# Delta-net mixer: keys squared first, the pair scales on VectorE, half of the block copies on GpSimd, and the diagonal copies placed behind the E blocks

## The chip, the cores and the metric

The program runs on one core of one Trainium2 chip. The metric is the device time of one launch in microseconds (us), from arrays in HBM to the output in HBM. The engines named below are TensorE (PE; PEld is its weight load), VectorE (DVE), ScalarE (ACT), GpSimd (POOL) and SyncE (SP), which issues the transfers of the weights.

## The reference, cut to what matters

Two layers are computed, each a feed-forward block, a mixer and another feed-forward block, with an RMS norm before and behind each. D is 1024, there are 256 tokens in float32. The mixer of layer 1, a gated delta-net with 8 key heads and 16 value heads of width 128 and chunks of 64, is where the change lies:

```
q, k, v = silu(causal_conv4(x @ w_in))           # per channel, width 4
q, k    = l2norm(q), l2norm(k)                   # x * rsqrt(sum(x*x) + 1e-6), each repeated for 2 value heads
q       = q * 128 ** -0.5
decay   = exp(g[:, None] - g[None, :]) below and on the diagonal, 0 above    (g = cumulative log decay)
a       = strict lower part of (beta * k @ k.T) * decay
t_inv   = inverse of (eye + a)                   # one 64 x 64 triangular inverse per chunk and head
u, w    = t_inv @ (v * beta), t_inv @ (k * beta * exp(g))
then chunk by chunk: v_new = u - w @ state; o = q_g @ state + qk @ v_new; state = decayed state + k_tail.T @ v_new
out     = (rms_norm(o) * silu(z)) @ w_out
```

The kernel squares and sums q and k per head for the l2 norms, forms k @ k.T and k @ q.T for all heads, scales them by beta over the key's squared norm and by the decay, works with chunks of 128 tokens (one token tile), and inverts the strict triangles of all 32 pairs of value head and token tile together. The 1e-6 under the norm of q is carried into the output's RMS norm (the tile eq).

## The kernel before, in words

Every weight arrives in units of 512 KB (128 x 1024 float32) through SP's queue into one of 3 raw buffers. Each unit is split: ACT copies it to a rounded high part (whi, L119) and DVE subtracts that from the raw data for the low part (wlo, L121), into one of 8 buffer pairs. A product in float32 is three matmuls: high by high, low by high, high by low. They run nearly back to back on PE from the first microsecond to the last, and the delta-net's side work runs beside and between them.

What stands where is set twice. While the program is written, Python generators ("chains": the heads' chain kq_chain, invert, scan, v_pair, z_chain) are advanced by a ticker that is called every few projection matmuls, with written-out delays (KQ_WAIT 3, INV_WAIT 37, V_WAIT 4 ticks). Then a scheduler in the framework fixes one queue for each engine, by its own estimate of costs and priorities; issue_after(x) asks it to place an instruction behind x. On the chip each queue runs strictly in that order, and instructions wait on semaphores for data and for free buffers. So an edit on one line can move rows of other lines.

The part that the change touches, in the order of time (span of the delta-net mixer some 660 to 900 us of the profile):

- Convolutions and SiLU of the 16 q and k channels blocks: L584 (ACT) and three L586 (DVE) each, then SiLU L573 (ACT) for a head's k and q together. Their tiles are called kq.
- kq_chain, for each of 4 groups of 2 key heads. For each head PE transposes q and k into one PSUM bank (L618) and multiplies k by k and q into another (L621); both banks come from a pool of 4, called acc, so each bank is reused two heads later. ACT reads the first bank with the copies ktok (L624) and k1 (L625, from kq) and four squares with a running sum (L630, output "junk", sums in kss). Then the pair scales: POOL adds EPS to the sums (L634), DVE takes the reciprocal (L636, rk), POOL multiplies it with beta for the two token tiles (L639, dsc). POOL also makes the square root nk (L654), eq (L656) and wt (L658).
- For each token tile DVE writes four scaled products (L645, tile KQ, which frees the product banks), 8 for a group. For each tile four block copies on ACT (L652) pick the 32 x 32 diagonal blocks of KQ into one big tile blk for the inversion; 32 copies in all, 8 for a group.
- invert, once all four groups are through: DVE transposes blk (L669), then 31 steps of two DVE operations (L677, L679) invert all 32 x 32 blocks together, and two DVE transposes (L681, L683) bring the results back. POOL then copies the inverted blocks into E (L699, with a memset L700) for half 0 and half 1, and 32 diagonal blocks into KQ (L689). PE, ACT assemble the larger inverses from them (L707, L711, L718, L719, L732, L739).
- Meanwhile the projection goes on with z and then v. The v pairs pass through convolution (L584, L586), SiLU and transposes on PE (L757), and scan uses the inverses.

Of the kernel before, what the change touches and what calls it, by code (L numbers as in the profile page):

```python
# [7 lines left out]
F32 = mybir.dt.float32  # L8
F32R = mybir.dt.float32r
AF = mybir.ActivationFunctionType  # L10
ALU = mybir.AluOpType
PSUM = bass.MemoryType.PSUM

P = 128
# [35 lines left out]
def trunk_kernel(ctx: ExitStack, tc: tile.TileContext, x, norm_g, w_gu, w_dn, sc_in, sc_cw, sc_out,  # L50
# [425 lines left out]
    def gdn_proj(xh, xl, mid):  # L476
# [128 lines left out]
        def kq_chain():  # L605

            for gi in range(NG):
                ss = sp.tile([P, NT, 2, 2], F32, name="kss", bufs=2)
                k1 = slab([P, 2, 2, P], F32, "kq1")
                pkq = []  # L610
                for i in range(2):
# [11 lines left out]
                    pkq.append(pk)  # L623
                    S.activation(ktok[:, kh, :], tp[:, 0, 0, :], AF.Copy)  # L624
                    S.activation(k1[:, i, :, :], kq[kh][:, :, P:], AF.Copy)  # L625
                    kq1[kh] = k1[:, i, :, :]
                    for t in range(NT):
                        for c in range(2):
                            junk = sp.tile([P, 512], mybir.dt.bfloat16, name="junk", bufs=1)
                            S.activation(junk[:, 0:P], tp[:, t, c, :], AF.Square, accum_out=ss[:, t, c, i:i + 1])  # L630
# [3 lines left out]
                G.tensor_scalar(ss, ss, EPS, None, ALU.add)  # L634
                rk = sp.tile([P, NT, 2], F32, name="rk", bufs=2)
                V.reciprocal(rk, ss[:, :, 0, :])  # L636
                dd = small(f"dsc{gi}", 8).rearrange("p (t n) -> p t n", t=NT)
                for t in range(NT):
                    G.tensor_tensor(dd[:, t, :].rearrange("p (k v) -> p k v", k=2),  # L639
                                    beta[:, t, 4 * gi:4 * gi + 4].rearrange("p (k v) -> p k v", k=2),  # L640
                                    rk[:, t, :].unsqueeze(2).broadcast_to([P, 2, 2]), ALU.mult)
                for t in range(NT):
# [5 lines left out]
                    for b in range(4):  # L648
                        r = slice(b * B32, (b + 1) * B32)
                        o = Ld[r, :, 8 * gi + t:8 * gi + t + 7:2].rearrange("p i v -> p v i")  # L650
                        i_ = m[r, :, 0, b * B32:(b + 1) * B32]
                        S.activation(o, i_, AF.Copy)  # L652
                n = small(f"nk{gi}", 4).rearrange("p (t n) -> p t n", t=NT)
                G.tensor_tensor(n, ss[:, :, 0, :], phalf.rearrange("p (t n) -> p t n", t=NT), ALU.pow)  # L654
                q = small(f"eq{gi}", 4).rearrange("p (t n) -> p t n", t=NT)
                G.tensor_scalar(q, ss[:, :, 1, :], 128.0 * EPS, None, ALU.mult)  # L656
# [10 lines left out]
        def invert():  # L667
# [17 lines left out]
            for gi in range(NG):  # L685
                for t in range(NT):
                    for b in range(4):
                        r = slice(b * B32, (b + 1) * B32)
                        G.tensor_copy(KQ[gi][t][r, :, 0, r], Yd[r, 8 * gi + t:8 * gi + t + 7:2, :])  # L689
            yield INV_WAIT  # L690
            for half in range(2):
# [3 lines left out]
                for gi in gis:  # L695
# [4 lines left out]
                    G.memset(E[gi][0:B32, :, B32:], 0.0)  # L700
# [355 lines left out]
```

## Time and profile before

| | us |
|---|---|
| three timed runs | 1131.48, 1131.45, 1130.69 |
| median | 1131.45 |
| profiled execution | 1128.42 |
| its span, first to last instruction | 1126.5 |
| PE busy in the span | 1100.2 |
| DVE, ACT, POOL busy | 749.9, 651.8, 88.8 |

The profiled execution lies 3.03 us below the median of the timed runs, and 1.92 us of it are outside the span. The mean granted PE clock is 0.995 of full speed. PE is busy 98% of the span, so time can only go where PE idles, or where it runs at a lower clock; a matmul's busy time overlaps the next one's, so rows of matmuls are read by their starts. In a timeline row the first number is the start, the second the length of the piece, "xN" the instructions in it, and the bracket is the idle time of the engine before it and what ended that.

### The profile page before, as it was taken

How to read it: one execution, taken by the hardware profiler on the slowest of the kernel's cores; microseconds unless marked ns; L12 is line 12 of the kernel's file. 1: busy time of each engine (PE TensorE's matmuls, PEld its weight loads, DVE VectorE, ACT ScalarE, POOL GpSimd, SP SyncE). 2: the span in 40 equal slices, each digit the busy share in tenths (PEclk: the TensorE clock that was granted, in tenths of full speed). 3: DMA queues.
4: the chain of work that ended last, by engine and by line, in shares of the span. 5: the costliest groups of instructions: out<-in, count | busy, mean ns of one | idle time of the engine just before them, and what ended most of it. 6: DMA issues, size and time to landing. Idle time of an engine off the chain costs nothing.

```text
span 1126.5 us, 16842 instructions
## 1 busy us (share of the span) xinstructions
PE 1100.2 (98%) x6284; PEld 942.4 (84%) x6284; DVE 749.9 (67%) x1140; ACT 651.8 (58%) x1201; POOL 88.8 (8%) x167
## 2 busy tenths in 40 slices
PE   9999999999999999999999999889899999999997
PEld 6888887888788888788888877778899887888886
DVE  7776735687777663577765468768946557767543
ACT  6666535545556653556664358784587645666432
POOL 0100000000200000010000012110141212000000
PEclk9999999999999999999999999999999999999999
DMA  8755555656566565576555653327332355655552
GB/s 271 244 185 190 191 166 167 225 180 198 182 223 204 171 206 165 163 229 209 189 185 169 193 185 113 94 94 227 114 129 76 131 168 168 213 199 190 185 168 75
DMA packets 55955, 198.12 MB, mean 176 GB/s; under 512 B 6721, under 2 KB 7233, under 8 KB 55874
## 3 DMA queue, kind: packets, MB, share of 16 engines
q1 hardware_dynamic: 55728, 196.99, 54.2%
q8 instruction: 49, 0.80, 0.3%
q14 instruction: 32, 0.26, 0.1%
q10 hardware_dynamic: 146, 0.07, 0.0%
HBM read 195.99 MB, written 1.05 MB: 175 GB/s over the span
## 4 chain that ended last, share of the span: by engine, by line
PE 81%; DVE 7%; ACT 5%; DMA 3%; issue 2%; POOL 2%; SPq 0%; DVEq 0%; POOLq 0%; ACTq 0%
PE mm L298 27%; PE mm L301 14%; PE acc L324 7%; PE acc L325 7%; PE acc L323 7%; PE mm L221 3%; PE mm L222 3%; PE mm L225 3%; DVE wlo L121 2%; ACT whi L119 1%; ACT blk L652 1%; DVE kq L586 1%; PE mm L176 1%; ACT junk L147 1%; DMA raw<-in_w_gu 1%
## 5 line engine op out<-in xcount | busy, mean ns | idle before, releaser
L121 DVE TENSOR_TENSOR wlo<-raw,whi 128x1024 fp32r<-128x1024 f32 (+2 forms) x362 | 437.5, 1220 | 240.2 <-ACT whi L119 201.5
L119 ACT ACTIVATE whi<-raw 128x1024 fp32r<-128x1024 f32 (+2 forms) x362 | 376.1, 1051 | 224.3 <-PE acc L325 104.6
L298 PE MATMUL mm<-x,whi 128*128 128x512 f32 x1312 | 329.4, 393 | 0.0
L298 PEld LDWEIGHTS mm<-x,whi 128*128 128x128 f32 x1312 | 235.9, 189 | 42.4
L301 PEld LDWEIGHTS mm<-x,wlo 128*128 128x128 f32 x1312 | 179.0, 190 | 12.8
L301 PE MATMUL mm<-x,wlo 128*128 128x256 f32 x1312 | 182.9, 282 | 0.0
L323 PE MATMUL acc<-whi,hb 128*128 128x512 f32 x352 | 136.5, 388 | 0.0
L324 PE MATMUL acc<-wlo,hb 128*128 128x512 f32 x352 | 135.6, 385 | 0.3 <-DVE wlo L121 0.3
L325 PE MATMUL acc<-whi,hb 128*128 128x512 f32 x352 | 135.3, 385 | 0.0
L308 ACT ACTIVATE corr<-mm 128x256 f32<-128x256 f32 x164 | 61.2, 376 | 67.4 <-PE mm L301 65.6
L221 PE MATMUL mm<-whi,x 128*128 128x512 f32 (+1 forms) x240 | 94.4, 394 | 0.9 <-ACT x L178 0.7
L222 PE MATMUL mm<-wlo,x 128*128 128x512 f32 (+1 forms) x240 | 94.2, 393 | 0.7 <-DVE wlo L121 0.7
L225 PE MATMUL mm<-whi,x 128*128 128x512 f32 (+1 forms) x240 | 87.8, 389 | 0.2 <-DVE x L179 0.2
L324 PEld LDWEIGHTS acc<-wlo,hb 128*128 128x128 f32 x352 | 66.2, 188 | 13.8 <-DVE wlo L121 0.8
L323 PEld LDWEIGHTS acc<-whi,hb 128*128 128x128 f32 x352 | 66.2, 188 | 13.1
L325 PEld LDWEIGHTS acc<-whi,hb 128*128 128x128 f32 x352 | 66.1, 188 | 13.2
L154 POOL TENSOR_SCALAR rstd<-ss 128x1 f32<-128x1 f32 x24 | 12.3, 513 | 786.1 <-ACT junk L147 786.1
L278 PE MATMUL mm<-x,whi 128*128 128x256 f32 x200 | 59.7, 299 | 2.0 <-DVE kq L586 2.0
L279 PE MATMUL mm<-x,whi 128*128 128x256 f32 x200 | 58.4, 292 | 0.0
L280 PE MATMUL mm<-x,wlo 128*128 128x256 f32 x200 | 57.9, 289 | 0.0
L222 PEld LDWEIGHTS mm<-wlo,x 128*128 128x128 f32 x240 | 45.2, 188 | 11.2 <-DVE wlo L121 2.9
L221 PEld LDWEIGHTS mm<-whi,x 128*128 128x128 f32 x240 | 45.2, 188 | 11.1 <-ACT x L178 2.7
(216 smaller groups left out, 1238.3 us busy)
## 6 DMA issues: line engine op xcount, KB each, us to landing
raw<-in_w_gu SPq DMA_DIRECT2D x176, 512.0 KB, 4.2
raw<-in_w_dn SPq DMA_DIRECT2D x88, 512.0 KB, 3.6
raw<-in_sc_in SPq DMA_DIRECT2D x24, 512.0 KB, 4.1
raw<-in_gdn_z SPq DMA_DIRECT2D x16, 512.0 KB, 3.9
raw<-in_gdn_v SPq DMA_DIRECT2D x16, 512.0 KB, 4.2
raw<-in_gdn_out SPq DMA_DIRECT2D x16, 512.0 KB, 3.7
gamma<-in_norm_g SPq DMA_DIRECT2D x11, 512.0 KB, 5.4
raw<-in_gdn_a SPq DMA_DIRECT2D x9, 512.0 KB, 4.4
```

The lines of the kernel that those rows point to most:

```text
L119: S.activation(hi[:, r], raw[:, r], AF.Copy)
L121: newest[0] = V.tensor_tensor(lo[:, r], raw[:, r], hi[:, r], ALU.subtract).ins
L221: PE.matmul(pt, lhsT=xh[:, t, k, :], rhs=hi, start=(k == 0), stop=False)
L222: PE.matmul(pt, lhsT=xh[:, t, k, :], rhs=lo, start=False, stop=False)
L225: PE.matmul(pt, lhsT=xl[:, t, j, :], rhs=part(j)[0], start=False, stop=(j == KD - 1))
L278: PE.matmul(ptile, lhsT=hi, rhs=h2, start=(k == 0), stop=False)
L298: PE.matmul(flat, lhsT=part(k, 0), rhs=xx[:, k].rearrange("p h t q -> p (h t q)"), start=(k == 0), stop=False)
L301: PE.matmul(flat[:, T:], lhsT=part(k, 1), rhs=xx[:, k, 0].rearrange("p t q -> p (t q)"), start=False, stop=(k == KD - 1))
L308: S.activation(c, pt[:, 1, :], AF.Copy)
L323: PE.matmul(o, lhsT=yh(c, t), rhs=hi[:, r], start=(c == 0), stop=False)
L324: PE.matmul(o, lhsT=yh(c, t), rhs=lo[:, r], start=False, stop=False)
L325: i = PE.matmul(o, lhsT=yl(c, t), rhs=hi[:, r], start=False, stop=(c == n - 1)).ins
```

## The change

Four edits, all in the delta-net mixer:

1. The four squares of a head stand ahead of the copies ktok and k1, and the two of the keys ahead of the two of the queries. The sums are laid out with the keys' in one piece.
2. The pair scales, that is the EPS for the keys, the reciprocal and the two multiplications by beta, are all on DVE. The EPS of the queries' sums goes into eq, which is one POOL operation as before; nk, the square root, now reads the keys' sums behind DVE's addition. nk, eq and wt stay on POOL.
3. Of the four block copies of a tile two stay on ACT (now L653) and two go to POOL (L655): 16 and 16 in all.
4. The 32 diagonal copies into KQ (L689, now L704) are written in each half, 16 behind that half's E copies, and are asked to stand behind the last memset of the half's E blocks.

```diff
--- before.py
+++ after.py
@@ -605,7 +605,7 @@
         def kq_chain():
 
             for gi in range(NG):
-                ss = sp.tile([P, NT, 2, 2], F32, name="kss", bufs=2)
+                ss = sp.tile([P, 2, NT, 2], F32, name="kss", bufs=2)
                 k1 = slab([P, 2, 2, P], F32, "kq1")
                 pkq = []
                 for i in range(2):
@@ -621,22 +621,22 @@
                         PE.matmul(pk[:, t, :, :], lhsT=kq[kh][:, 0, t * P:(t + 1) * P],
                                   rhs=kq[kh][:, :, t * P:(t + 1) * P], start=True, stop=True)
                     pkq.append(pk)
+                    for c in range(2):
+                        for t in range(NT):
+                            junk = sp.tile([P, 512], mybir.dt.bfloat16, name="junk", bufs=1)
+                            S.activation(junk[:, 0:P], tp[:, t, c, :], AF.Square, accum_out=ss[:, c, t, i:i + 1])
                     S.activation(ktok[:, kh, :], tp[:, 0, 0, :], AF.Copy)
                     S.activation(k1[:, i, :, :], kq[kh][:, :, P:], AF.Copy)
                     kq1[kh] = k1[:, i, :, :]
-                    for t in range(NT):
-                        for c in range(2):
-                            junk = sp.tile([P, 512], mybir.dt.bfloat16, name="junk", bufs=1)
-                            S.activation(junk[:, 0:P], tp[:, t, c, :], AF.Square, accum_out=ss[:, t, c, i:i + 1])
                     yield 1
                 while dec[1][gi] is None:
                     yield 1
-                G.tensor_scalar(ss, ss, EPS, None, ALU.add)
+                V.tensor_scalar(ss[:, 0], ss[:, 0], EPS, None, ALU.add)
                 rk = sp.tile([P, NT, 2], F32, name="rk", bufs=2)
-                V.reciprocal(rk, ss[:, :, 0, :])
+                V.reciprocal(rk, ss[:, 0])
                 dd = small(f"dsc{gi}", 8).rearrange("p (t n) -> p t n", t=NT)
                 for t in range(NT):
-                    G.tensor_tensor(dd[:, t, :].rearrange("p (k v) -> p k v", k=2),
+                    V.tensor_tensor(dd[:, t, :].rearrange("p (k v) -> p k v", k=2),
                                     beta[:, t, 4 * gi:4 * gi + 4].rearrange("p (k v) -> p k v", k=2),
                                     rk[:, t, :].unsqueeze(2).broadcast_to([P, 2, 2]), ALU.mult)
                 for t in range(NT):
@@ -649,11 +649,14 @@
                         r = slice(b * B32, (b + 1) * B32)
                         o = Ld[r, :, 8 * gi + t:8 * gi + t + 7:2].rearrange("p i v -> p v i")
                         i_ = m[r, :, 0, b * B32:(b + 1) * B32]
-                        S.activation(o, i_, AF.Copy)
+                        if b < 2:
+                            S.activation(o, i_, AF.Copy)
+                        else:
+                            G.tensor_copy(o, i_)
                 n = small(f"nk{gi}", 4).rearrange("p (t n) -> p t n", t=NT)
-                G.tensor_tensor(n, ss[:, :, 0, :], phalf.rearrange("p (t n) -> p t n", t=NT), ALU.pow)
+                G.tensor_tensor(n, ss[:, 0], phalf.rearrange("p (t n) -> p t n", t=NT), ALU.pow)
                 q = small(f"eq{gi}", 4).rearrange("p (t n) -> p t n", t=NT)
-                G.tensor_scalar(q, ss[:, :, 1, :], 128.0 * EPS, None, ALU.mult)
+                G.tensor_scalar(q, ss[:, 1], EPS, 128.0 * EPS, ALU.add, ALU.mult)
                 w = small(f"wt{gi}", 4)
                 G.tensor_tensor(w, etail[:, 4 * gi:4 * gi + 4], dd[:, 0, :], ALU.mult)
                 Dsc[gi], nk[gi], eq[gi], wt[gi] = dd, n, q, w
@@ -682,11 +685,6 @@
             Yd = row("blk").rearrange("p (a b) -> p a b", a=B32)
             V.transpose(Yd.rearrange("p h i -> p i h"), X)
             T1 = row("blk").rearrange("p (a b) -> p a b", a=B32)
-            for gi in range(NG):
-                for t in range(NT):
-                    for b in range(4):
-                        r = slice(b * B32, (b + 1) * B32)
-                        G.tensor_copy(KQ[gi][t][r, :, 0, r], Yd[r, 8 * gi + t:8 * gi + t + 7:2, :])
             yield INV_WAIT
             for half in range(2):
                 hs = slice(16 * half, 16 * half + 16)
@@ -697,7 +695,13 @@
                     for b in range(2):
                         r = slice(b * B32, (b + 1) * B32)
                         G.tensor_copy(E[gi][r, :, r], Xd[r, 8 * gi:8 * gi + 8, :])
-                    G.memset(E[gi][0:B32, :, B32:], 0.0)
+                    placed = G.memset(E[gi][0:B32, :, B32:], 0.0).ins
+                for gi in gis:
+                    for t in range(NT):
+                        for b in range(4):
+                            r = slice(b * B32, (b + 1) * B32)
+                            with tc.issue_after(placed):
+                                G.tensor_copy(KQ[gi][t][r, :, 0, r], Yd[r, 8 * gi + t:8 * gi + t + 7:2, :])
                 pt = side_bank().rearrange("p a (b c) -> p (a b) c", c=B32)
                 for x in range(16):
                     ht = 16 * half + x
```

The lines behind the edits are numbered anew: squares L627, ktok L628, k1 L629, scaled products still L645 in the queue below, inversion's transpose L672, its steps L680 and L682, E copies L697. Three places of the queues show what the scheduler makes of it.

First DVE at the pair scales of the first group (heads 0 and 1; their product banks are acc_6740 and acc_6800, KQ_6831 and KQ_6840 the two token tiles, kq_6753 a later head's convolution). Before:

```order
L121 TENSOR_TENSOR wlo_7087<-raw_7084,whi_7086 128x1024
L121 TENSOR_TENSOR wlo_7143<-raw_7140,whi_7142 128x1024
L586 SCALAR_TENSOR_TENSOR kq_6753<-mm_6677,gcw_6224,kq_6753 128x255
L636 RECIPROCAL rk_6826<-kss_6549 128x4
L586 SCALAR_TENSOR_TENSOR kq_6753<-mm_6782,gcw_6224,kq_6753 128x255
L586 SCALAR_TENSOR_TENSOR kq_6753<-mm_6677,gcw_6224,kq_6753 128x254
L645 SCALAR_TENSOR_TENSOR KQ_6831<-acc_6740,dsc0_6828,dec_6622 128x256
L586 SCALAR_TENSOR_TENSOR kq_6753<-mm_6677,gcw_6224,kq_6753 128x253
L645 SCALAR_TENSOR_TENSOR KQ_6831<-acc_6740,dsc0_6828,dec_6622 128x256
L645 SCALAR_TENSOR_TENSOR KQ_6831<-acc_6800,dsc0_6828,dec_6622 128x256 x2
L645 SCALAR_TENSOR_TENSOR KQ_6840<-acc_6740,dsc0_6828,dec_6627 128x256 x2
```

With the change (L645 is the same line in both):

```order
L634 TENSOR_SCALAR kss_6549<-kss_6549 128x4
L636 RECIPROCAL rk_6826<-kss_6549 128x4
L639 TENSOR_TENSOR dsc0_6828<-beta_6233,rk_6826 128x4 x2
L645 SCALAR_TENSOR_TENSOR KQ_6831<-acc_6740,dsc0_6828,dec_6622 128x256 x2
L645 SCALAR_TENSOR_TENSOR KQ_6840<-acc_6740,dsc0_6828,dec_6627 128x256 x2
L645 SCALAR_TENSOR_TENSOR KQ_6831<-acc_6800,dsc0_6828,dec_6622 128x256
L586 SCALAR_TENSOR_TENSOR kq_6753<-mm_6677,gcw_6224,kq_6753 128x255
L645 SCALAR_TENSOR_TENSOR KQ_6831<-acc_6800,dsc0_6828,dec_6622 128x256
L586 SCALAR_TENSOR_TENSOR kq_6753<-mm_6677,gcw_6224,kq_6753 128x254
L645 SCALAR_TENSOR_TENSOR KQ_6840<-acc_6800,dsc0_6828,dec_6627 128x256
L586 SCALAR_TENSOR_TENSOR kq_6753<-mm_6677,gcw_6224,kq_6753 128x253
L645 SCALAR_TENSOR_TENSOR KQ_6840<-acc_6800,dsc0_6828,dec_6627 128x256
```

The two weight splits that stood ahead of the group's products (wlo_7087, wlo_7143) now come behind all eight of them, with the next convolution rows, and the EPS addition, which waits for ACT's squares, stands where they stood. The four products on the first bank come first.

Second PE at the products of the heads 2 and 3 (transposes L618, products L621; kq_6590 and kq_6599 are the heads). Before, the transposes of head 3 stand 22 matmuls of the projection behind head 2's products:

```order
L278 MATMUL mm_6927<-x2_5783,whi_6778 128x256
L279 MATMUL mm_6927<-x2_5783,whi_6778 128x256
L280 MATMUL mm_6927<-x2_5783,wlo_6779 128x256
L278 MATMUL mm_7090<-x2_5783,whi_7086 128x256
L618 MATMUL acc_6904<-ident_81,kq_6599 128x128 x4
L279 MATMUL mm_7090<-x2_5783,whi_7086 128x256
L280 MATMUL mm_7090<-x2_5783,wlo_7087 128x256
L278 MATMUL mm_7090<-x2_5783,whi_7086 128x256
L279 MATMUL mm_7090<-x2_5783,whi_7086 128x256
L280 MATMUL mm_7090<-x2_5783,wlo_7087 128x256
L621 MATMUL acc_6909<-kq_6599 128x256 x2
L278 MATMUL mm_7090<-x2_5783,whi_7086 128x256
```

With the change they follow directly, and the products four rows later:

```order
L618 MATMUL acc_6874<-ident_81,kq_6590 128x128 x4
L621 MATMUL acc_6879<-kq_6590 128x256 x2
L618 MATMUL acc_6904<-ident_81,kq_6599 128x128 x4
L278 MATMUL mm_6927<-x2_5783,whi_6760 128x256
L279 MATMUL mm_6927<-x2_5783,whi_6760 128x256
L280 MATMUL mm_6927<-x2_5783,wlo_6761 128x256
L278 MATMUL mm_6927<-x2_5783,whi_6766 128x256
L621 MATMUL acc_6909<-kq_6599 128x256 x2
L279 MATMUL mm_6927<-x2_5783,whi_6766 128x256
L280 MATMUL mm_6927<-x2_5783,wlo_6767 128x256
L278 MATMUL mm_6927<-x2_5783,whi_6766 128x256
L279 MATMUL mm_6927<-x2_5783,whi_6766 128x256
```

Head 3's transposes and products moved ahead by 22 and 23 rows. As the banks are reused in turn, its transposes wait for the last reader of acc_6795, now the copy ktok of head 1, and its products for the last L645 on acc_6800. The heads 4 and 5 moved ahead of some projection matmuls likewise, and between the two products of head 4 (acc_6989) stand 24 matmuls; the last head's transposes stand 3 matmuls of 512 columns later than before.

Third DVE at the last group and the inversion's start. Before:

```order
L121 TENSOR_TENSOR wlo_7161<-raw_7158,whi_7160 128x1024
L121 TENSOR_TENSOR wlo_7404<-raw_7401,whi_7403 128x1024
L121 TENSOR_TENSOR wlo_7410<-raw_7407,whi_7409 128x1024
L636 RECIPROCAL rk_7208<-kss_7103 128x4
L645 SCALAR_TENSOR_TENSOR KQ_7213<-acc_7110,dsc3_7210,dec_6664 128x256 x2
L645 SCALAR_TENSOR_TENSOR KQ_7213<-acc_7188,dsc3_7210,dec_6664 128x256 x2
L645 SCALAR_TENSOR_TENSOR KQ_7222<-acc_7110,dsc3_7210,dec_6669 128x256 x2
L645 SCALAR_TENSOR_TENSOR KQ_7222<-acc_7188,dsc3_7210,dec_6669 128x256 x2
L121 TENSOR_TENSOR wlo_7416<-raw_7413,whi_7415 128x1024
L669 STREAM_TRANSPOSE blk_7252<-blk_6238 128x1024
L121 TENSOR_TENSOR wlo_7422<-raw_7419,whi_7421 128x1024
```

With the change:

```order
L121 TENSOR_TENSOR wlo_7378<-raw_7375,whi_7377 128x1024
L634 TENSOR_SCALAR kss_7103<-kss_7103 128x4
L121 TENSOR_TENSOR wlo_7384<-raw_7381,whi_7383 128x1024
L636 RECIPROCAL rk_7208<-kss_7103 128x4
L639 TENSOR_TENSOR dsc3_7210<-beta_6233,rk_7208 128x4 x2
L645 SCALAR_TENSOR_TENSOR KQ_7213<-acc_7110,dsc3_7210,dec_6664 128x256 x2
L645 SCALAR_TENSOR_TENSOR KQ_7213<-acc_7188,dsc3_7210,dec_6664 128x256 x2
L645 SCALAR_TENSOR_TENSOR KQ_7222<-acc_7110,dsc3_7210,dec_6669 128x256 x2
L645 SCALAR_TENSOR_TENSOR KQ_7222<-acc_7188,dsc3_7210,dec_6669 128x256 x2
L121 TENSOR_TENSOR wlo_7390<-raw_7387,whi_7389 128x1024
L672 STREAM_TRANSPOSE blk_7252<-blk_6238 128x1024
```

One weight split (wlo_7384) now stands between the EPS addition and the reciprocal, where before it had been done ahead of the reciprocal; the transpose waits for the last block copies of ACT and of POOL.

## The prediction

> **What bounds the kernel now.** I read the page's busy shares first, then PE's timeline in the stretch that the change touches, then the granted clock in windows, then the other engines' timelines ahead of each of PE's waits, and last the waits and the groups.
>
> ```profile
> PE 1100.2 (98%) x6284; PEld 942.4 (84%) x6284; DVE 749.9 (67%) x1140; ACT 651.8 (58%) x1201; POOL 88.8 (8%) x167
> ```
>
> PE is the bound on the whole. So the change can gain only what PE loses near it. PE's timeline shows these losses (the bracket at a row's end):
>
> ```profile
> 729.23 0.66 PE L618 MATMUL acc<-ident,kq 128*128 128x128 f32 x4 [0.36 <-ACT junk L630]
> 732.18 1.13 PE L621 MATMUL acc<-kq 128*128 128x256 f32 x4 [1.71 <-DVE KQ L645]
> 738.22 0.66 PE L618 MATMUL acc<-ident,kq 128*128 128x128 f32 x4 [0.53 <-ACT kq L573]
> 746.69 1.12 PE L618 MATMUL acc<-ident,kq 128*128 128x128 f32 x4 [3.06 <-ACT kq L573]
> 747.60 1.91 PE L621 MATMUL acc<-kq 128*128 128x256 f32 x4
> ...
> 794.53 1.12 PE L757 MATMUL mm<-ident,yb 128*128 128x128 f32 x4 [3.41 <-ACT yb L573]
> 812.06 1.20 PE L707 MATMUL acc<-blk,KQ 32*32 32x32 f32 x64 [0.18 <-DVE blk L681]
> ```
>
> The waits in the heads' chain are 0.36, 1.71, 0.53 and 3.06 us. Later there are 3.41 us ahead of the first v pair's transposes, and 0.18 at the start of the assembly of the inverses. Two of them are followed by a slower clock (PEclk is the column behind the five busy times):
>
> ```profile
> 748.00:752.00 4.00, 4.00 (x15) 3.23 (x14) 0.53 (x2) 2.51 (x11) 2.10 (x7) 0.75 0.77 269
> 795.00:798.00 3.00, 3.00 (x17) 3.00 (x16) 3.00 (x9) 1.99 (x4) 0.00 (x0) 0.54 0.56 167
> ```
>
> The clock is 0.75 and 0.54 there, and the matmuls show it: the last head's four transposes take 1.12 us instead of the 0.66 of 738.22, its four products 1.91 instead of the 1.13 of 732.18. The 3.06 us wait thus costs another 1.2 (0.46 and 0.78), the 3.41 about 1.4 (3 us at 0.54; an estimate). The wait of 1.71 slowed nothing.
>
> Who is late at 746.69 and 812.06? Two windows, ahead of and behind the start of the inversion (columns: length, then busy time of PE, PEld, DVE, ACT, POOL):
>
> ```profile
> 714.00:747.00 33.00, 27.16 (x184) 24.41 (x184) 24.84 (x52) 31.08 (x96) 6.55 (x18) 0.99 0.23 70
> 758.00:812.00 54.00, 50.29 (x327) 46.12 (x326) 50.21 (x103) 29.12 (x40) 0.00 (x0) 0.97 0.58 177
> ```
>
> From 714 to 747 ACT is busy for 31.08 of 33 us: the heads' chain goes at ACT's pace. From 758 to 812 DVE is busy for 50.21 of 54: inversion, weight splits and the v convolutions go at DVE's pace, and PE arrives at L707 0.18 us too early, so both are just in balance there. The end of the stretch moves when the inversion's transpose (L669, 758.02) moves. The link between the two windows, from the last head's SiLU to that transpose:
>
> ```profile
> 746.02 0.62 ACT L573 ACTIVATE kq<-kq 128x512 f32<-128x512 f32 x1
> 749.39 0.19 ACT L630 ACTIVATION_READ_ACCUMULATOR junk<-acc 128x1 f32 x1
> 749.67 0.24 POOL L634 TENSOR_SCALAR kss<-kss 128x8 f32<-128x8 f32 x1 [12.43 <-ACT junk L630]
> 749.94 0.18 DVE L636 RECIPROCAL rk<-kss 128x4 f32<-128x4 f32 x1 [2.43 <-POOL kss L634]
> 751.65 3.23 DVE L645 SCALAR_TENSOR_TENSOR KQ<-acc,dsc,dec 128x256 f32<-128x256 f32 x8 [1.53 <-POOL dsc L639]
> 754.79 1.22 DVE L121 TENSOR_TENSOR wlo<-raw,whi 128x1024 fp32r<-128x1024 f32 x1
> 753.34 1.85 ACT L652 ACTIVATE blk<-KQ 32x128 f32<-32x128 f32 x4 [0.82 <-DVE KQ L645]
> 755.21 1.06 ACT L119 ACTIVATE whi<-raw 128x1024 fp32r<-128x1024 f32 x1
> 756.18 1.80 ACT L652 ACTIVATE blk<-KQ 32x128 f32<-32x128 f32 x4
> 758.02 1.25 DVE L669 STREAM_TRANSPOSE blk<-blk 128x1024 f32<-128x1024 f32 x1 [2.01 <-ACT blk L652]
> ```
>
> SiLU, PE's transposes at 746.69, squares, the scales on POOL and DVE, eight products, block copies with a weight conversion between them, transpose: the whole link runs in series.
>
> **The change part by part.** The prices:
>
> ```profile
> L652 ACT ACTIVATE blk<-KQ 32x128 f32<-32x128 f32 x32 | 13.8, 430 | 2.3 <-DVE KQ L645 2.0
> L630 ACT ACTIVATE junk<-acc 128x128 bf16<-128x128 f32 x32 | 8.8, 276 | 0.6
> L630 ACT ACTIVATION_READ_ACCUMULATOR junk<-acc 128x1 f32 x32 | 6.4, 201 | 0.0
> L639 POOL TENSOR_TENSOR dsc<-beta,rk 128x4 f32<-128x4 f32 x8 | 1.4, 201 | 0.3
> L654 POOL TENSOR_TENSOR nk<-kss,phalf 128x4 f32<-128x4 f32 x4 | 4.2, 1044 | 0.3
> ```
>
> (a) *Last head earlier: 2.8 us.* Before 746.02 ACT carries out 24 of the 32 block copies; in the new queue only 12 of ACT's 16 stand ahead of that SiLU. Twelve copies of 0.430 us are 5.2 us of ACT time, less one weight conversion (1.06 us, the row of 755.21) that now stands ahead of it too: 4.1 us at most. The floor is 0: the head's convolution also needs PE's projection and DVE. The heads' products, pulled ahead on PE, now wait for ACT's ktok copies (put behind the squares) and for the scaled products of the group before. Following the new queue row by row with the durations above I get waits of some 0.5, 0.85, 1.3 and 0.15 us, 2.8 in all, for the 2.6 us (0.36, 1.71 and 0.53) that they replace. PE's own feed is therefore no earlier, and I take two thirds of ACT's 4.1, 2.8.
>
> The first group's scaled products come much earlier by their new place:
>
> ```profile
> 714.86 1.23 DVE L121 TENSOR_TENSOR wlo<-raw,whi 128x1024 fp32r<-128x1024 f32 x1 [1.01 <-ACT whi L119]
> 716.58 1.23 DVE L121 TENSOR_TENSOR wlo<-raw,whi 128x1024 fp32r<-128x1024 f32 x1 [0.50 <-ACT whi L119]
> 717.26 0.66 POOL L634 TENSOR_SCALAR kss<-kss 128x8 f32<-128x8 f32 x1 [14.02 <-ACT junk L630]
> 719.68 0.48 DVE L645 SCALAR_TENSOR_TENSOR KQ<-acc,dsc,dec 128x256 f32<-128x256 f32 x1 [0.63 <-POOL dsc L639]
> ```
>
> The scales begin at 717.26 and the products at 719.68; now they stand ahead of both weight splits, and with the squares first I put them at about 714.7. The splits (queued behind them: four convolution rows and the next group's scales) go to about 720. PE uses their low parts only some 50 rows behind head 3's products, so nothing is late by it at first; what it costs if that slack is gone is the rival below.
>
> (b) *From the last head's transposes to its last square: 0.8 us.* Now 746.69 to 749.58 (POOL's addition begins 0.09 behind it), 2.9 us. With about a quarter of the wait left the clock stays up, so the transposes give 0.46 back; ktok goes behind the squares, which is under 0.3. Floor 0, ceiling 1.2.
>
> (c) *From the last square to the first scaled product: 0.15 us.* Now 751.65 - 749.58 = 2.07 us: POOL carries out nk (1.044 us) and eq between its addition and its multiplication. On DVE the addition, the reciprocal (0.18) and two multiplications (0.201 on POOL, taken as much) are some 0.8. That would be 1.25 less, but the new queue puts a weight split of 1.22 between the first two. If its data are late, it costs more: I let this term go down to -1.2, and up to 1.25 if the split is not yet in the way.
>
> (d) *The eight products* stay at 3.23 us; nk moves beside them and costs nothing, as POOL has nothing else due.
>
> (e) *From the last product to the transpose: 1.9 us.* Now 758.02 - 754.88 = 3.14 us, in which ACT makes four copies and the conversion. Now two copies remain on each engine behind the last product, 0.86 us on ACT, on POOL by the nearest rows:
>
> ```profile
> L689 POOL COPY KQ<-blk x32: 283/287/1190, 815.4 to 827.6; 32x128 f32<-32x128 f32 x32
> L699 POOL COPY E<-blk x8: 387/393/1335, 812.1 to 830.1; 32x256 f32<-32x256 f32 x8
> 814.19 1.29 POOL L699 COPY E<-blk 32x256 f32<-32x256 f32 x1
> 828.77 2.67 POOL L699 COPY E<-blk 32x256 f32<-32x256 f32 x2
> 828.63 2.56 DVE L121 TENSOR_TENSOR wlo<-raw,whi 128x1024 fp32r<-128x1024 f32 x2 [3.93 <-ACT whi L119]
> ```
>
> A copy of 32 x 128 on POOL takes 0.287 us as a rule and 1.19 at most. The E copies take 0.39, and 1.29 to 1.335 where a weight split runs on DVE. The new queue has a split of 1.22 us between the last product and the transpose in any case, so the transpose comes 1.2 us behind the last product: 3.14 - 1.2. Bounds: both copies at 1.19 give 0.76, and no delay by the split gives 2.3.
>
> The Trainium skill speaks against this edit: by "SBUF — State Buffer", section "Who interferes with whom", a DVE instruction with two SBUF inputs, such as the weight split, shares a read port with a POOL instruction that reads SBUF, and the one that comes second blocks until the first is through. The trace agrees (1.29 beside a split, 0.39 alone). By that rule the first of the two copies waits out the split and the second follows: the transpose would come some 0.6 us (two copies of 0.287) later than in my sum, by the row alone it would not.
>
> (f) *From the transpose on: carried in full.* DVE has 54 us of work, 93% busy, and each of its splits frees the raw buffer for the next load, so the chain slides as a whole. PE, earlier by (a) and by the clock, still waits some 3 us for the first v pair, which hides nothing. One split less stands behind the transpose (up to 1.2 us more gain; taken at 0, since it waits for its load).
>
> (g) *Diagonal copies in halves: 0.*
>
> ```profile
> 815.44 12.48 POOL L689 COPY KQ<-blk 32x128 f32<-32x128 f32 x32
> ```
>
> Half 1's E copies (828.77) stand behind 32 copies now and behind 16 then, some 6 us earlier. The 16 that go behind end where the E copies end now, about 832, and the solves that read them come later. PE shows no wait for E there, so I count nothing; if these copies were on the path, up to 0.7.
>
> Sum: 2.8 + 0.8 + 0.15 + 1.9 = 5.65 us. The profiled execution goes from 1128.42 to 1122.8 by it. Its time is 3.03 below the median of the timed runs, so the forecast is 1131.45 - 5.7 = **1125.8 us**. By the ends of the terms this forecast reaches from 1122.5 to 1129.2 (gains of 9 and of 2.3).
>
> **The rivals.**
>
> *The loads set the pace behind the transpose: 1130.6.*
>
> ```profile
> ACT whi L119 <- DMA raw<-in_gdn_v: 9.1, 9, 1.5
> ```
>
> ACT waits nine times, 9.1 us in all, for v weights to land. If those loads can't start earlier, the first v pair comes at 789 to 794 as before, PE's 3.41 us wait grows by what was won ahead, and only a split's share, below 1 us, is left. For it: the row. Against it: a load starts when DVE frees its buffer, and DVE's 93%.
>
> *PE alone becomes the bound: 1122.0.* PE's six waits are 9.25 us, with the slow clock 11.9. But DVE has to be as early: 5.65 and the 3.8 us that it idles from 758 to 812 are 9.4. For it: less ACT work also brings conversions earlier. Against it: new waits on the banks.
>
> *Slower: 1134.6.* The pulled-ahead products are the place. PE's queue is in order; head 3's products wait for eight scaled products of the first group, the heads 4 and 5 for ktok copies, each behind four squares (0.276 and 0.201 us each). If two of these waits grow to the 3.06 us of the last head's, each with its slow clock of 1.2, PE loses 8.6 us for the 2.6 removed. (a) becomes -6.0, the rest of the sum brings 2.85 back, and 3.15 are lost. It decides from 5.45 us of new waits on. For it: two such waits come close together. Against it: ACT has 5 us less to do in that stretch, and my count has half as much.
>
> **How the numbers follow.** A measurement of this kernel tells 0.2%, 2.3 us, from no change. Chances: the forecast 0.61, the loads 0.17, PE alone 0.10, slower 0.12. Nearly all of the first and the third are faster: 0.70. The loads' case is no change: 0.17 with a little of the first taken off for values near 1129; slower 0.13. The range of 8 in 10 takes in the forecast and the loads' case, and most of PE alone: 1121.0 to 1132.0.
>
> **What would show it.** In the profile of the changed kernel: the first L645 near 715 (a); PE's wait ahead of the last head's transposes at or below 1 us, near 744, with a full clock behind (a, b); the transpose near 752.3 (c to e), where 755 or later makes (a) wrong; POOL's block copies at 0.29 us, and near 1.2 only beside splits; L707 near 806.5 (f): if the transpose is early but L707 still comes at 811 to 812, the loads' case holds. PE's waits between 718 and 732 adding up to over 5 us would show the slower case.

## The result and the profile after

The changed kernel takes 1120.28 us (median of four executions, 1117.82 to 1122.17) against 1131.45: the ratio is 0.9901, with a 95% interval of 0.9887 to 0.9915. It is faster by 11.2 us, about twice the 5.7 forecast, and the time lies 0.7 us below the range. A second measurement on another occasion gave 1118.36 (1117.75 to 1119.31) against 1130.24, a ratio of 0.9897 (0.9882 to 0.9912).

The profiled execution took 1121.48 us, its span is 1119.8. PE's timeline of the changed kernel, the rows that answer to those of before, and the first wait of the mixer, which stands ahead of the change's reach and is there in both (before: 707.50, 1.97 us; in both profiles a slow stretch of the granted clock follows it, with 0.63 from 708 to 712 us before and 0.72 now):

```profile
709.49 0.39 PE L278 MATMUL mm<-x,whi 128*128 128x256 f32 x1 [1.98 <-DVE kq L586]
...
726.16 0.70 PE L621 MATMUL acc<-kq 128*128 128x256 f32 x2 [0.97 <-ACT ktok L628]
...
743.93 0.66 PE L618 MATMUL acc<-ident,kq 128*128 128x128 f32 x4
744.43 1.03 PE L621 MATMUL acc<-kq 128*128 128x256 f32 x4
...
787.61 0.66 PE L761 MATMUL mm<-ident,yb 128*128 128x128 f32 x4 [1.98 <-ACT yb L573]
```

This profile is 1.99 us later at its first mixer wait than that of before (709.49 against 707.50), so times are compared less 1.99. Of the waits 0.36, 1.71, 0.53 and 3.06 only one of 0.97 is left. The last head's transposes start without a wait, at full clock (0.66 and 1.03 us instead of 1.12 and 1.91). The first v pair's wait fell from 3.41 to 1.98, and the one at the start of the assembly (L707, now L711) is gone. From the first mixer wait to the end of the span it is 410.3 us instead of 419.0: 8.7 us less.

The link from the last SiLU to the inversion's transpose, from the timelines of ACT, DVE and POOL of the changed kernel:

```profile
743.25 0.64 ACT L573 ACTIVATE kq<-kq 128x512 f32<-128x512 f32 x1
745.58 0.17 DVE L634 TENSOR_SCALAR kss<-kss 128x4 f32<-128x4 f32 x1 [1.04 <-ACT junk L627]
745.68 1.23 DVE L121 TENSOR_TENSOR wlo<-raw,whi 128x1024 fp32r<-128x1024 f32 x1
745.89 1.88 POOL L657 TENSOR_TENSOR nk<-kss,phalf 128x4 f32<-128x4 f32 x1 [4.62 <-DVE kss L634]
746.83 0.17 DVE L636 RECIPROCAL rk<-kss 128x4 f32<-128x4 f32 x1
747.03 0.24 DVE L639 TENSOR_TENSOR dsc<-beta,rk 128x4 f32<-128x4 f32 x2
747.30 3.23 DVE L645 SCALAR_TENSOR_TENSOR KQ<-acc,dsc,dec 128x256 f32<-128x256 f32 x8
749.09 0.89 POOL L655 COPY blk<-KQ 32x128 f32<-32x128 f32 x2 [0.75 <-DVE KQ L645]
750.44 1.22 DVE L121 TENSOR_TENSOR wlo<-raw,whi 128x1024 fp32r<-128x1024 f32 x1
750.59 1.82 POOL L655 COPY blk<-KQ 32x128 f32<-32x128 f32 x2 [0.61 <-DVE KQ L645]
750.89 0.90 ACT L653 ACTIVATE blk<-KQ 32x128 f32<-32x128 f32 x2
752.43 1.25 DVE L672 STREAM_TRANSPOSE blk<-blk 128x1024 f32<-128x1024 f32 x1 [0.78 <-ACT zs L573]
```

The SiLU is 4.8 us earlier (743.25 - 1.99 against 746.02), the transpose 7.6 (752.43 - 1.99 against 758.02). The transpose's bracket names zs, which it does not read. zs and POOL's last copy both end at 752.41, ACT's copies at 751.79, so it is POOL's copies that the transpose waits for; in experiments 3, 6, 7, 8 and 10 to 12 the bracket names them.

The two windows again, shifted with the work (columns: length, then PE, PEld, DVE, ACT, POOL busy, granted clock, DMA):

```profile
716.00:749.00 33.00, 32.03 (x210) 28.96 (x209) 29.49 (x72) 30.30 (x98) 14.12 (x24) 1.00 0.40 118
752.43:804.41 51.98, 50.01 (x327) 46.33 (x326) 48.72 (x101) 27.00 (x38) 1.32 (x3) 0.97 0.56 175
```

PE is busy 32.03 of 33 us in the first now. ACT is still at 30.30, for more of the heads' chain lies in the window. From the transpose to the end of the first transposing back (L681, now L684) it is 51.98 us instead of 53.98.

### The profile page after: what moved, and what is told of

The parts are those of the page before. It is cut to its first block, busy times and chain, and to the rows that moved or that the text cites. A ratio compares the mean times of both kernels' runs of the same rounds, so it can differ in the third digit from the quotient of the medians.

```text
span 1119.8 us, 16865 instructions
## 1 busy us (share of the span) xinstructions
PE 1099.2 (98%) x6284; PEld 942.5 (84%) x6284; DVE 750.7 (67%) x1152; ACT 645.2 (58%) x1185; POOL 94.6 (8%) x171
```

## The experiments

All times below are medians, with the kernel before measured on the same chip. It had 1130.89 us beside the first four, 1130.24 beside the next four, 1131.10 beside the last four. The ratios with their 95% intervals are those on record; they take in all executions of both kernels and differ a little from the quotient of the two medians.

**1. The changed kernel with all block copies on ACT.**

```diff
-                        if b < 2:
-                            S.activation(o, i_, AF.Copy)
-                        else:
-                            G.tensor_copy(o, i_)
+                        S.activation(o, i_, AF.Copy)
```

> The changed kernel with all 32 block copies back on ScalarE, the other three edits kept. Theory A (ScalarE's time sets the pace of the heads' chain, and the twelve copies taken off it are the gain): most of the gain goes, 1126 to 1129 us, a wait of 2 to 3 us ahead of the last head's transposes is back, and the inversion's transpose comes 4 to 6 us later than with the change. Theory B (the early pair scales free the product banks and so PE, and the copies matter only at the very end): 1121.5 to 1123 us, the last head's transposes come without a wait of over 1 us, and only the 1.2 us from the last product to the transpose are lost.

Measured: 1127.10 us, ratio 0.9975 (0.9965 to 0.9984). PE's waits in the heads' chain:

```profile
724.71 0.66 PE L618 MATMUL acc<-ident,kq 128*128 128x128 f32 x4 [1.84 <-ACT ktok L628]
...
746.90 1.11 PE L618 MATMUL acc<-ident,kq 128*128 128x128 f32 x4 [3.51 <-ACT kq L573]
```

The wait ahead of the last head is back with 3.51 us, and the transposes run at a slow clock (1.11 us). From the first mixer wait (709.28) to the last SiLU (746.22) it takes 36.9 us. In the second profile of the changed kernel, which like this one had no slow stretch behind that first wait, it is 32.3. A part of the 4.6 us between them is the new wait of 1.84 us and the slow stretch behind it (0.67 from 724 to 728 us). Theory A holds and B falls.

**2. The scales' POOL operations back on POOL.**

```diff
-                V.tensor_scalar(ss[:, 0], ss[:, 0], EPS, None, ALU.add)
+                G.tensor_scalar(ss[:, 0], ss[:, 0], EPS, None, ALU.add)
...
-                    V.tensor_tensor(dd[:, t, :]...
+                    G.tensor_tensor(dd[:, t, :]...
```

> The changed kernel with the EPS addition and the two multiplications by beta back on GpSimd (the addition for the keys alone, the reciprocal on VectorE as ever). Theory A: at most the 0.3 us measured for the last group and something in the groups before, 1120 to 1122 us. Theory B: the products come 1 to 2 us later in each group, the banks come free later, PE waits over 2 us more in the heads' chain: 1123 to 1127 us.

Measured: 1122.26 us, ratio 0.9929 (0.9913 to 0.9944). That is 2.0 us above the first measurement of the changed kernel and 3.9 above the second, just outside both ranges; of the 11 to 12 us of gain 8.6 are left. In the heads' chain PE waits 0.18 and 1.15 us, only 0.4 more than with the change. But the last SiLU (744.65) comes 35.3 us behind the first mixer wait (709.32) instead of 33.8, both with a slow stretch behind that wait, the transpose 9.5 us behind the SiLU instead of 9.2, and the wait for the first v pair grew:

```profile
789.55 1.12 PE L761 MATMUL mm<-ident,yb 128*128 128x128 f32 x4 [3.81 <-ACT yb L573]
```

Its 3.81 us are followed by a slow clock, as in the kernel before. So the early scales bring the chain of DVE and ACT forward, and with it the inversion; what they do by freeing banks for PE, B's mechanism, is small.

**3 and 6. Squares behind ktok and k1 again**, measured twice.

```diff
+                    S.activation(ktok[:, kh, :], tp[:, 0, 0, :], AF.Copy)
+                    S.activation(k1[:, i, :, :], kq[kh][:, :, P:], AF.Copy)
                     for c in range(2):
                         for t in range(NT):
                             ... square ...
-                    S.activation(ktok[:, kh, :], tp[:, 0, 0, :], AF.Copy)
-                    S.activation(k1[:, i, :, :], kq[kh][:, :, P:], AF.Copy)
```

> The changed kernel with the squares behind the copies ktok and k1 again (keys still ahead of queries). Theory A: the same work on ScalarE in another order, 1120 to 1121.5 us. Theory B: the scales of each group start 0.7 us later, 1121.5 to 1124 us. On the other hand the transposes' bank comes free with the squares again and not with ktok, which would take away PE's wait of 0.97 us: 1119.5 us if that decides.

> The changed kernel with the squares behind ktok and k1 again, as in the third experiment (1117.4 us there). If the order of the squares costs the changed kernel something: 1116.5 to 1118.5 us and 1.5 to 3.5 us below the changed kernel beside it. If the third experiment only met fewer slow stretches of the clock: 1119 to 1121 us, within 1 us of the changed kernel.

Measured: 1117.36 us (ratio 0.9890, 0.9869 to 0.9911), then 1118.64 (0.9900, 0.9878 to 0.9922) beside the changed kernel's 1118.36. The first looked like a gain by taking the edit out; beside the changed kernel nothing is left of it. PE's wait in the heads' chain is 0.94 instead of 0.97 and ends on the squares instead of ktok: it did not go away. The transpose even comes 0.7 to 0.8 us earlier without this edit, counted from the first mixer wait (40.7 us in experiment 3 against 41.4 in experiment 5, both without a slow stretch behind that wait; 42.1 in experiment 6 against 42.9 in the first profile, both with one), but the time does not show it. Putting the squares ahead of the copies is worth nothing that these runs can tell. The other half of the first edit, the keys' squares ahead of the queries', is kept in both.

**4. Diagonal copies ahead of both halves' E copies again** (the loop of the fourth edit back at its old place, without the request to stand behind the memset).

> The changed kernel with the 32 diagonal copies ahead of both halves' E copies as before. Both theories: 1120 to 1121 us, no difference that can be measured; if half 1's E copies set the path with the inversion now early, 0.5 to 6 us more and a wait of PE ahead of half 1's first products.

Measured: 1118.82 us, ratio 0.9903 (0.9885 to 0.9921). No difference from the changed kernel.

**5. The changed kernel once more.**

> The changed kernel itself once more, beside the next three on the same chip. If the part of the gain that the profiles don't show (8.7 us in the two profiles from the first wait at 707 us on, 11.2 us between the medians) is the state of the granted clock behind PE's waits and the start of the launch, which differ from one execution to the next, the median is 1119 to 1121.5 us and the profiled execution's time goes with its mean clock as in the four executions so far (1122.17 us at 0.993, 1121.48 at 0.995, 1119.08 at 0.998, 1117.82 at 0.999).

Measured: 1118.36 us, 0.6 below the range, and this profiled execution took 1117.75 us at a mean clock of 0.999, in line with the four before. It has the waits of the first profile, 1.96 us at 708.82 and 1.75 us at 785.22 (instead of 1.98 and 1.98), but the clock differs. Windows behind these two waits, in the first profile of the changed kernel:

```profile
708.00:712.00 4.00, 2.51 (x13) 2.52 (x14) 4.00 (x7) 2.33 (x11) 0.00 (x0) 0.72 0.16 16
712.00:716.00 4.00, 4.00 (x29) 3.95 (x29) 2.23 (x6) 1.84 (x8) 0.00 (x0) 0.85 0.69 244
788.00:792.00 4.00, 4.00 (x24) 4.00 (x23) 4.00 (x11) 2.35 (x5) 0.00 (x0) 0.57 0.42 131
```

and in the second:

```profile
708.00:712.00 4.00, 3.18 (x26) 3.18 (x27) 3.96 (x7) 2.17 (x11) 0.00 (x0) 1.00 0.25 65
712.00:716.00 4.00, 4.00 (x33) 3.89 (x32) 3.63 (x12) 4.00 (x12) 1.21 (x2) 1.00 0.56 204
784.00:788.00 4.00, 2.78 (x24) 2.78 (x25) 4.00 (x11) 3.11 (x7) 0.00 (x0) 1.00 0.28 68
```

The clock is 0.72, 0.85 and 0.57 in the one, 1.00 in the other. So a wait of two microseconds costs its own length in one execution and some 1.5 us more in the next (33.8 us instead of 32.3 from the first of these waits to the last SiLU).

**7. Only the block copies**, on the kernel before.

```diff
-                        S.activation(o, i_, AF.Copy)
+                        if b < 2:
+                            S.activation(o, i_, AF.Copy)
+                        else:
+                            G.tensor_copy(o, i_)
```

> The kernel before with only the third edit: two of four block copies on GpSimd. Theory A (ScalarE's time sets the pace of the heads' chain): the larger part of the gain comes with this edit alone, 1122 to 1126 us, and the wait of 3.06 us ahead of the last head's transposes shrinks to under 1 us. If the copies need the early scales beside them (GpSimd holds the scale operations and the copies in one queue, so each group's scales could wait behind the copies of the group before): 1127 to 1131 us.

Measured: 1122.20 us, ratio 0.9929 (0.9912 to 0.9945). Eight of the changed kernel's 11 to 12 us come from this edit alone. PE's timeline at the last head and at the first v pair:

```profile
743.69 0.66 PE L618 MATMUL acc<-ident,kq 128*128 128x128 f32 x4 [0.32 <-ACT kq L573]
...
789.86 1.11 PE L760 MATMUL mm<-ident,yb 128*128 128x128 f32 x4 [3.36 <-ACT yb L573]
```

The 3.06 us are down to 0.32. From the first mixer wait (710.61) to the last SiLU (743.02) it takes 32.4 us, as the whole change does (32.3 in its second profile; neither has a slow stretch there). What the other edits add lies behind: the v pair still waits 3.36 us here.

**8. V pairs' transposes later**, on the kernel of experiment 3.

```diff
-V_WAIT = 4
+V_WAIT = 6
```

> The kernel of the third experiment with V_WAIT at 6 ticks instead of 4, so that the transposes of each v pair stand some 2.9 us later in PE's queue. Theory (what bounds the changed kernel from the transpose to the assembly is again PE, with the wait for the first v pair the last one of size): the wait of 1 to 2 us ahead of these transposes goes, and with it the slow clock behind it where it comes, 1114 to 1117 us. If VectorE's chain is the bound there, the wait turns up ahead of the first products of the assembly and the time stays at 1116.5 to 1119 us.

Measured: 1119.57 us, ratio 0.9907 (0.9891 to 0.9924). The wait ahead of L761 is gone, and this one stands at the assembly instead:

```profile
803.49 1.20 PE L711 MATMUL acc<-blk,KQ 32*32 32x32 f32 x64 [1.26 <-DVE blk L684]
```

It is 1.26 us. With PE's own wait out of the way DVE's chain is the bound at the assembly, as the prediction had it; the wait can be moved, and the time does not fall below that of experiments 3 and 6.

**9. Only the scales**, on the kernel before: the key layout of the sums, with the addition and the two multiplications on DVE. The keys' squares stand ahead of the queries' here too.

> The kernel before with only the second edit: the pair scales on VectorE, keys' sums in one piece. If the edits add up as the runs so far suggest (copies alone 8 us, the changed kernel without them 3.1 to 3.8 us, without the scales 2 to 3.9 us worse): 1126 to 1128.5 us, with the wait of over 3 us ahead of the last head's transposes still there. If the scales do nothing without the copies, since ScalarE sets the pace: 1129.5 to 1131 us.

Measured: 1127.23 us, ratio 0.9960 (0.9945 to 0.9975), with 3.79 us of wait ahead of the last head still there. The scales on DVE, with this order of the squares, bring 3.9 us by themselves.

**10. Copies and scales only**, with the squares behind ktok and k1 and the diagonal copies as before. The keys' squares stay ahead of the queries'.

> The second and third edit alone, squares behind ktok and k1 and diagonal copies ahead of all E copies as before. If the first and fourth edit are worth nothing: 1117.5 to 1120.5 us, as the changed kernel. If the first edit's early squares are needed for the early scales: 1121 to 1123 us.

Measured: 1119.89 us, ratio 0.9900 (0.9883 to 0.9916): the changed kernel's time. The two edits add up, 8.0 and 3.9 alone and 11.2 together. The squares ahead of the copies and the place of the diagonal copies bring nothing. What the keys' squares ahead of the queries' are worth was not tested apart from the scales.

**11. Three of four block copies on POOL** (`if b < 1` instead of `if b < 2`).

> The changed kernel with three of four block copies on GpSimd, 8 more off ScalarE (3.4 us). Theory A, with its end: PE no longer waits for the last head, so ScalarE's time is no longer what counts there, and the three copies behind the last product on GpSimd come 0.3 to 1.2 us later: 1118 to 1121 us, no gain, and 1121 to 1123 us if these copies are blocked beside the weight split (0.4 us each alone, up to 1.3 beside it). If ScalarE's time still sets the pace: 1115 to 1117 us.

Measured: 1118.89 us, ratio 0.9883 (0.9865 to 0.9901). No gain beyond the changed kernel that can be told. In the profile the last SiLU does come earlier, 32.4 us behind the first mixer wait instead of 33.8 (both with a slow stretch behind that wait), and PE's wait of 0.97 us is gone. But from the SiLU to the transpose it takes 9.6 us instead of 9.2, with POOL's copies as the last thing waited for, and what is left does not show in the time.

**12. One more decay tile on ACT.**

```diff
-GUACT = 1
+GUACT = 2
```

> The changed kernel with a second of the eight decay tiles made on ScalarE (4 instructions of 0.4 us) and one less on VectorE (0.6 us). It aims at the wait of 1.97 us ahead of the first matmul at 709 us, where VectorE's convolutions are late, and at the slow stretch of the clock that follows in some executions. If VectorE's backlog is the cause: the wait shrinks to about 1.4 us and the time to 1117.5 to 1119.5 us. If ScalarE's convolution instructions are pushed out by as much as VectorE wins: no change, 1118.5 to 1121 us.

Measured: 1116.74 us (1116.14 to 1117.68), ratio 0.9871 (0.9856 to 0.9885). This is the lowest median of all. The wait of 1.97 us at 709 went altogether, more than the 0.6 us that were moved. PE's waits of this profile in the heads' chain and at the v pairs add up to 3.0 us, of which the first v pair's is 0.49:

```profile
724.66 1.13 PE L621 MATMUL acc<-kq 128*128 128x256 f32 x4 [1.06 <-ACT ktok L628]
734.62 0.66 PE L618 MATMUL acc<-ident,kq 128*128 128x128 f32 x4 [0.60 <-ACT kq L573]
784.06 0.66 PE L761 MATMUL mm<-ident,yb 128*128 128x128 f32 x4 [0.49 <-ACT yb L573]
```

Its interval lies below that of the changed kernel's first measurement and overlaps that of the second by a hair, so some 2 to 3 us of gain over the changed kernel are likely, and not certain. Why the wait vanished whole, when the DVE work that was taken away is a third of it, the traces show: the matmul waits for convolution rows on DVE (L586), and these meet POOL's eight selects of the decay tiles (L559). In the changed kernel:

```profile
698.84 6.39 POOL L559 TENSOR_SCALAR_AFFINE_SELECT dec<-dec 128x512 f32<-128x512 f32 x8 [12.88 <-ACT dec L558]
698.86 8.62 DVE L586 SCALAR_TENSOR_TENSOR kq<-craw,gcw,kq 128x253 f32<-128x253 f32 x14
```

and here:

```profile
698.76 5.59 DVE L586 SCALAR_TENSOR_TENSOR kq<-craw,gcw,kq 128x253 f32<-128x253 f32 x14
700.50 10.81 POOL L559 TENSOR_SCALAR_AFFINE_SELECT dec<-dec 128x512 f32<-128x512 f32 x8 [13.73 <-ACT dec L558]
```

The same fourteen rows take 8.62 us when POOL's first select starts just ahead of them, most of them 0.85 us each, and 5.59 us when they start first, 0.47 us each; then it is POOL that is held, for 4.35 us in its longest select. In all thirteen other profiles the selects start first, by 0.01 to 0.03 us, and the rows take 8.60 to 8.62 us. One more decay tile on ACT makes POOL's selects later, and the 3.0 us so won cover the wait. That the order of the two starts decides was read from these traces, not tried by itself.

## Why the prediction was too small

The path was the one forecast: ACT's time, the last head, the transpose, DVE's chain. The direction was right, and the slower rival did not come. Two terms were wrong, (a) and (f), and so was the step from the profile to the median. In the coordinates of the profile before:

| step | forecast | measured | from |
|---|---|---|---|
| (a) last head's SiLU earlier | 2.8 | 4.8 | 746.02 to 741.26 |
| (b) to the EPS addition | 0.8 | 1.3 | 749.67 to 743.59, 6.1 in all |
| (c) to the first product | 0.15 | 0.3 | 751.65 to 745.31 |
| (e) to the transpose | 1.9 | 1.2 | 758.02 to 750.44, 7.6 in all |
| (f) to the end of L681 | 0 | 2.0 | 812.00 to 802.42, 9.6 in all |
| end of the span | 5.65 | 8.7 | 419.0 to 410.3 behind the first mixer wait |

The transpose at 752.43 in its own profile looks like the 752.3 that was forecast, but that is chance: this profile is 1.99 us later, and less that the transpose is 1.9 us earlier than forecast. Two figures of the prediction's working don't come out. The lower end of its gains, 2.3, is not the sum of the terms' lower ends, which is -0.4 (0, 0, -1.2 and 0.76); and the 0.15 of (c) is 0.05 by its own numbers (2.07 less 0.8 less 1.22).

**Step (a) failed by 2.0 us.** It set ACT's ceiling at 4.1 and took two thirds, since the pulled-ahead products were to wait for 2.8 us and PE's feed would be no earlier. The new waits measured 0.97 instead of 2.8 (0.36, 1.71 and 0.53 went, with the 0.17 at 721.62), so PE's feed was 1.8 us earlier than taken and ACT's whole ceiling was realised: from the first mixer wait to that SiLU its work fell from 34.40 to 30.16 us, and its idle time from 4.12 to 3.60. Experiments 1 and 7 show that this term is the copies': 32.4 us from the first mixer wait to the last SiLU with them alone, 36.9 without them, the new wait and its slow stretch included.

**Step (b)** was 0.5 us too small: the addition, now on DVE, waits for the keys' squares only, which end at 745.47, while the queries' end at 746.28.

**Step (e) was 0.7 us too large**, by the rule that the prediction set beside it. The last two POOL copies took 1.82 us beside the weight split (750.59, 750.44), and the two of the tile before 0.89 us alone (749.09). They end at 752.41, and the transpose starts at 752.43. The first of the two copies lasted past the split's end at 751.66 (L655's longest copy took 1.35 us, its median one 0.42), and the square root beside the other split shows the same (745.89: 1.88 us, where it took 1.04 before). The Trainium skill, "SBUF — State Buffer", section "Who interferes with whom", says this of a DVE instruction with two SBUF inputs and a POOL instruction that reads SBUF; the trace agrees. The price for the copies is set too low as well: their median on POOL is 0.42 us, not the 0.287 of the diagonal copies.

**Step (f) failed by 2.0 us.** The split that no longer stands behind the transpose was named, and taken at 0. DVE's part from the transpose to the end of L681 has 17 splits instead of 18, and 48.72 us of work instead of 50.21 (the windows of both profiles); its idle time fell from 3.79 to 3.26. Of the work 1.2 us are the split and 0.45 are one convolution row (19 instead of 20). The idle time went with the clock: in the changed kernel's second profile, with no slow stretch here, the same part takes 50.7 us with 48.63 of work. So the 1.5 us of work are the change's; the remaining 0.5 are less than the 1.25 by which this part differs between the two executions of the changed kernel. At the end of the span the 9.6 us of DVE's chain don't count in full: PE reaches the assembly 0.5 us behind L684's end (804.94 against 804.41), and PE's part, with 8.9 at the v pair and 8.7 at the end, is the smaller gain. By the profiles, then, the case "PE alone becomes the bound" (9.4 us) came nearer than the forecast; but experiment 8 shows that DVE's chain is close behind.

**Step (g)** was right at nothing (experiments 4 and 10). The loads' rival fell: the first v pair came 8.9 us earlier.

**The median.** The profiles give 8.7 us, the medians 11.2. The prediction carried the whole difference of 3.03 us between the profiled execution of before and its median over to the changed kernel. It doesn't carry over: the changed kernel's first profiled execution lies 1.2 us above its median. The profile of before was an early one. At the mixer's first transposes (675.21) it was 1.6 us ahead of the changed kernel's (676.82), in work that both do alike. In the thirteen other profiles of this study that point lies between 674.62 and 678.44, with a median of 676.94. The clock is the likely home of much of the rest. Both profiles have a mean clock of 0.995, but the kernels as a rule do not. Beside the experiments the kernel before ran 27 more times, at clocks of 0.991 to 0.996 with a mean of 0.9940, and the changed kernel's eight executions have 0.993 to 0.999 with a mean of 0.9974. A straight line through the eight gives 0.7 us less for each 0.001 of the clock, one through the 27 gives 0.5, so the difference of the two means is worth 1.7 to 2.4 us (an estimate), most of the missing 2.5. This fits the waits. The kernel before has four waits of 1.7 us or more in the mixer, the changed one has two, and the fourteen profiles have 30 such waits between 676 and 840 us. All 6 of over 3 us were followed by a slow stretch, 14 of the 24 between 1.7 and 2.5 us were, and none of 1.3 us or less. How the 2.5 us divide between the start and the clock stays open, as the start was recorded in the profiles only.

The Trainium skill, "TensorE: Matmul & The Clock Gate", Part 1, says that the window over which PE's activity is judged runs freely, so the moment of a switch depends on where in it the work falls. That one and the same wait is followed by a slow clock in one execution and not in another agrees with it. Why a wait of 2 us is enough, no run here shows.

## What to carry to other kernels

Where one engine is busy for 31 of 33 us ahead of PE's waits, count work taken off it nearly in full, until PE's waits are gone (experiment 11): a third of it, held back here for new waits that were only argued, was one of the two largest misses. Price work that a scheduler moves across the point where the pace changes hands (here the transpose) instead of setting it at nothing. Look at which of two engines that slow each other starts first: the 0.6 us of experiment 12 turned that round and won 3.0 us of DVE's time. And where PE's waits switch its clock in some executions only, a single profile is an uncertain anchor for the median, by up to 3 us here.

## What the runs showed that was not expected

A wait of 1.97 us is enough for a slow stretch of the clock (0.72 and 0.85 in the windows behind it), and the same wait leaves the clock at 1.00 in another execution. DVE's convolution rows of 0.47 us took 0.85 beside POOL's selects when these started first, and held one of them for 4.35 us when they themselves did (experiment 12). A block copy of 32 x 128 out of KQ took a median of 0.42 us on POOL, as much as on ACT (0.43), where the diagonal copy of the same shape into KQ takes 0.29 (minimum, median and maximum in ns, from the changed kernel's rows by line):

```profile
L655 POOL COPY blk<-KQ x16: 400/423/1349, 719.9 to 752.0; 32x128 f32<-32x128 f32 x16
L704 POOL COPY KQ<-blk x32: 281/288/1190, 807.9 to 822.1; 32x128 f32<-32x128 f32 x32
```

POOL's square root of 128 x 4 was held from 1.04 to 1.88 us beside a weight split.
